# Two more raw buffers for the up weights of the context half of a SwiGLU feed-forward

## The chip, the cores and the metric

The program runs on one core of one Trainium2 chip. The core has a TensorE (PE in the profile, with its weight loads shown as PEld), a VectorE (DVE), a ScalarE (ACT), a GpSimd (POOL) and a SyncE (SP), which work on their own instruction queues and meet at semaphores, and 16 DMA engines that move data between HBM and on-chip SBUF. The metric is the device time of one execution in microseconds (us); lower is better.

## The reference

A backbone trunk of two layers over 1024 latent tokens and a prefix of 256 context tokens, model width 1024. Each layer has a mixing part (grouped attention beside a bidirectional Mamba-2 scan, one shared input and one shared output projection) and a SwiGLU feed-forward of width 2816. In the first layer both streams are updated; in the second only the latent one. The part that matters here is the feed-forward:

```python
D_FF = -(-8 * D_MODEL // (3 * 256)) * 256          # 2816

def swiglu(h, w_gate, w_up, w_down):
    return (jax.nn.silu(h @ w_gate) * (h @ w_up)) @ w_down
...
        if update_ctx:
            x_ctx = x_ctx + g1_c * rmsnorm(m_c, norm_mix_post[l])
            f_c = rmsnorm(x_ctx, norm_ffn_pre[l]) * (1.0 + sc2_c) + sh2_c
            x_ctx = x_ctx + g2_c * rmsnorm(swiglu(f_c, w_gate[l], w_up[l], w_down[l]), norm_ffn_post[l])
```

All inputs are float32.

## The kernel before

**Arithmetic.** Every matrix product in float32 is made of three PE passes over numbers in a shorter float format. An operand is split into hi, the rounded number, and lo, what is left. `split` does this with two instructions: hi is an ACT copy (a CAST, L114), lo is a subtraction (L115) on DVE or POOL. `mm3` then issues hi by hi, hi by lo and lo by hi (L224, L225, L226).

**Weights.** `plan` lists all weight units of the program in the order in which PE wants them, and `pump` emits them. `unit` (from L119) makes one: it takes a raw tile `raw_t` of 128 x 1024 floats (4 KB in each partition) from the pool `raw`, which has **two buffers** used in turn, lets SP load it by DMA (L125), takes a split tile `w_t` from the pool `wr`, which has five buffers, and splits the one into the other. `pump` emits unit i only after PE's use of unit i-5 has been written down (`RING = 5`). Which engine makes lo is chosen in `pump`: DVE for keys that hold "z" or "u", POOL for most of the others, gate units among them.

**The stage.** The context part of the first layer's feed-forward is `ctx_gateup` (L1061 on). For each of 22 column blocks `ff` it multiplies one gate unit and one up unit by the context tile `hc`: 8 x 3 matmuls of 128x256 for each unit, 48 for a block, 1056 in all. The units come in the order g0, u0, g1, u1 and so on, so with two raw buffers used in turn the gate units fall on the one and the up units on the other. Then ACT takes silu of the gate result (L1073), DVE multiplies by the up result (L1074), the product is split into `xt` and stored to `hid` by an ACT-issued DMA (L1077). After each block `next(fill, None)` issues one step of `fill_c`, the preparation of the latent half: it flips two latent token tiles (`flip_steps`, L398 to L408), loads rows of the residual stream (`row_halves`, L376, tile `s2t`), and forms the sums of `quads` (L1005 to L1032), 32 PE transposes (L1012) with ACT, DVE and POOL work and DMAs of its own. When block 21 is done, `ffn` makes the latent half of the same layer; its weights are again raw tiles (`wblock`, L205 loads, L213 to L216 sums on DVE, then splits).

**Memory.** Pools are opened and closed as a stack. `accp` is the pool of this stage and of the latent half that follows; it lies where the pools of the attention lay, which are closed by then. `grp` has one buffer with tag `grow`; in the attention's output projection it holds the gate row (read by L828), later in `ffn` the tile `head_g` of block 3, and after it the gate row of the down projection.

**Order.** The code is written in one sequence. A scheduler with a model of time then moves instructions within each engine's queue, and places the waits for buffers. So a change in buffers can change the order on every engine, also far behind the place of the edit.

Of the kernel before, what the change touches and what calls it, by code (L numbers as in the profile page):

```python
# [9 lines left out]
F32 = mybir.dt.float32  # L10
# [7 lines left out]
P = 128  # L18
# [36 lines left out]
class Trunk:  # L55
    def __init__(self, nc, tc, es, I, out):
# [24 lines left out]
        d = lambda name, shape: self.dr.tile(shape, F32, name=name)  # L81
# [11 lines left out]
        self.hf_d = [d(f"hf{l}", [KT // 2, 2, P, 512]) for l in range(DEPTH)]  # L93
        self.b22_d = d("b22", [KT // 4, 2, P, 512])
        self.hid_d = [d(f"hid{l}", [NFF, P, 2, TOK]) for l in range(DEPTH)]
        self.cols, self.last_x = {}, {}


    def psw(self):
# [16 lines left out]

    RING = 5

    def unit(self, parts, shape, dst=None, eng=None):  # L119
        nc = self.nc  # L120
        n = int(np.prod(shape))
        r = self.raw.tile([P, 1024], F32, tag="raw", name="raw_t")
        rv = r[:, :n].rearrange("p (a b) -> p a b", a=shape[0])
        for sl, ap in parts:
            nc.sync.dma_start(rv[:, :, sl], ap)  # L125
        w = dst if dst is not None else self.wr.tile([P, 2, 1024], F32R, tag="w", name="w_t")
        self.split(w[:, 0, :n], w[:, 1, :n], r[:, :n], eng)
        return w[:, :, :n].rearrange("p s (a b) -> p s a b", a=shape[0])
# [43 lines left out]
    def pump(self):  # L172
        while self.nemit < len(self.seq):
            i = self.nemit
            if i >= self.RING and self.seq[i - self.RING][0] not in self.freed:
                return
            key, parts, shape = self.seq[i]
            if shape is None:
                w = self.wr.tile([P, 2, 1024], F32R, tag="w", name="w_t")
                for j, b in enumerate(parts):  # L180
                    self.wblock(w[:, :, j * 512:(j + 1) * 512], *b)
                self.U[key] = w
                self.nemit += 1
                continue
            self.U[key] = self.unit(parts, shape, None, None if key[1] in "zu" or i < 4 or key[2:] == (0, 0) or len(key) == 4 and key[:3] == (1, "d", 2) and key[3] % 2 else self.nc.gpsimd)
            self.nemit += 1

    def free(self, *key):
# [891 lines left out]
    def ffn(self, l, B, fill, accp=None, xs0=None, xs1=None):  # L1080
        nc = self.nc

        def mul(p, ff, a, b):
            n, j = self.wpos[l, ff, a]
            w = self.U[l, "w", n][:, :, j * 512:(j + 1) * 512]
            for k in range(4):
                s = slice(k * P, (k + 1) * P)
                self.mm3(p, (w[:, 0, s], w[:, 1, s]), (B[b][:, k, 0], B[b][:, k, 1]), k == 0, k == 3)
            if j:
                self.free(l, "w", n)  # L1090
# [11 lines left out]
        def head(ff):  # L1102
            if ff == 3:
                g = self.grp.tile([P, D], F32, tag="grow", name="head_g")
                x1, sa = g[:, 0:512], g[:, 512:1024]
            else:
                x1, sa = [accp.tile([P, 512], F32, name=f"head{i}") if ff == 2 else self.s2() for i in range(2)]
            a = self.psw()
            mul(a, ff, "A11", "B11")
            nc.scalar.copy(x1, a)  # L1110
            a = self.psw()
            mul(a, ff, "A12", "B21")
            fill()
            tt(sa, x1, a, op=ALU.add)
            nc.scalar.activation(sa, sa, AF.Silu)
            st[ff] = x1, sa
# [37 lines left out]
        if heads:  # L1154
            for _ in self.quads(l, xs0, 0, B):
                pass
            head(0)
            self.pre_scale(xs1)
            head(1)
            for _ in self.quads(l, xs1, 1, B):  # L1160
                pass
            head(2)
            head(3)
            third(0)
# [67 lines left out]
def emit(nc, tc, I, out, dump=None):  # L1232
    with ExitStack() as es:
        k = Trunk(nc, tc, es, I, out)
# [18 lines left out]
        for l in range(DEPTH):  # L1253
# [62 lines left out]
            with tc.tile_pool(name=f"acc{l}", bufs=1, reuse_waits="tile") as accp:  # L1316
                if l == 0:
                    B = {}

                    def fill_c():  # L1320
                        fl[2]()
                        yield
                        xs = [k.row_halves(t, 0) for t in (6, 7)]
                        B.update(k.blocks(accp))
                        yield
                        for i in range(2):
                            k.pre_scale(xs)
                            yield
                            for _ in k.quads(0, xs, i, B):
                                yield  # L1330
                            if i == 0:
                                xs = [k.row_halves(t, 0) for t in (8, 9)]
                                yield

                    fc = fill_c()
                    k.ctx_gateup(0, fc)
                    drain(fc)
# [57 lines left out]
```

## Time and profile before

| what | value |
|---|---|
| three runs, us | 3227.97 (median), 3227.72, 3238.06 |
| profiled execution, us | 3234.53, of which its span is 3232.7 |
| granted PE clock, mean over the span | 0.973 |
| `ctx_gateup`, first to last matmul of `hc` by `w_t` | 855.6 to 1030.5 us |

The profiled execution is one run of its own; its span is counted from its first to its last recorded instruction. A row of the windows view gives for one stretch the length, the busy time of each engine with its number of instructions (x), the granted PE clock as a share of full speed, the busy share of the 16 DMA engines and the rate at which they moved data. A row of a timeline gives start, duration, engine, line, operation and out<-in; in square brackets stands the idle time before and what ended it. The chain of waits goes back from the last instruction of a stretch, at each step to what released it. Names are the kernel's own, without buffer numbers; `SPq` and `ACTq` are DMAs being issued.

### The profile page before, as it was taken

How to read it: one execution, taken by the hardware profiler on the slowest of the kernel's cores; microseconds unless marked ns; L12 is line 12 of the kernel's file. 1: busy time of each engine (PE TensorE's matmuls, PEld its weight loads, DVE VectorE, ACT ScalarE, POOL GpSimd, SP SyncE). 2: the span in 40 equal slices, each digit the busy share in tenths (PEclk: the TensorE clock that was granted, in tenths of full speed). 3: DMA queues.
4: the chain of work that ended last, by engine and by line, in shares of the span. 5: the costliest groups of instructions: out<-in, count | busy, mean ns of one | idle time of the engine just before them, and what ended most of it. 6: DMA issues, size and time to landing. Idle time of an engine off the chain costs nothing.

```text
span 3232.7 us, 44982 instructions
## 1 busy us (share of the span) xinstructions
PE 3041.5 (94%) x16147; PEld 2517.7 (78%) x16147; DVE 1665.7 (52%) x3093; ACT 1410.9 (44%) x2595; POOL 1663.6 (51%) x1529
## 2 busy tenths in 40 slices
PE   6899899999888999999998998899999899999997
PEld 4677688888787777778876778788888688888885
DVE  2557556777553655553021156759665766554003
ACT  4433337667653333332143344337666633333232
POOL 4327465555654444444476643755444555554653
PEclk8899899999999999999999999999999899999999
DMA  6267553222565554446566515653222443336766
GB/s 229 71 216 229 188 171 105 84 66 72 170 207 179 169 189 156 171 170 235 181 227 230 169 51 166 216 172 113 66 66 79 137 131 117 111 110 209 237 241 213
DMA packets 372703, 510.66 MB, mean 158 GB/s; under 512 B 25400, under 2 KB 258520, under 8 KB 372224
## 3 DMA queue, kind: packets, MB, share of 16 engines
q1 hardware_dynamic: 292912, 385.09, 37.9%
q10 hardware_dynamic: 79568, 122.69, 10.3%
q8 instruction: 128, 2.10, 0.3%
q14 instruction: 95, 0.78, 0.1%
HBM read 384.71 MB, written 122.99 MB: 157 GB/s over the span
## 4 chain that ended last, share of the span: by engine, by line
PE 73%; DMA 9%; DVE 6%; POOL 5%; ACT 3%; issue 3%; SPq 0%; ACTq 0%; DVEq 0%; POOLq 0%
PE ps_w L224 11%; PE ps_w L225 11%; PE ps_w L226 11%; PE ps_s L224 7%; PE ps_s L225 7%; PE ps_s L226 7%; PE ps_w L912 5%; PE ps_w L905 4%; PE ps_s L883 4%; POOL w_t L115 3%; DMA raw_t<-in_w_down 2%; DMA raw_t<-in_w_up 2%; ACT w_t L114 1%; PE ps_w L275 1%; PE ps_w L755 1%
## 5 line engine op out<-in xcount | busy, mean ns | idle before, releaser
L115 POOL TENSOR_TENSOR w_t<-raw_t,w_t 128x512 fp32r<-128x512 f32 (+2 forms) x430 | 795.7, 1861 | 834.3 <-ACT w_t L114 806.1
L114 ACT CAST w_t<-raw_t 128x512 fp32r<-128x512 f32 (+2 forms) x490 | 389.3, 810 | 774.4 <-PE ps_s L226 240.5
L884 DVE TENSOR_SCALAR_CACHE_REDUCE att_a<-ps_s 128x512 f32<-128x512 f32 (+1 forms) x400 | 227.0, 586 | 138.4 <-PE ps_s L883 128.1
L892 POOL TENSOR_SCALAR att_a<-att_a,att_st 128x1280 f32<-128x1280 f32 (+1 forms) x144 | 181.7, 1264 | 152.3 <-DVE att_st L891 84.2
L225 PE MATMUL ps_w<-w_t,hid_ring 128*128 128x512 f32 x523 | 207.5, 397 | 8.6 <-POOL w_t L115 8.6
L226 PE MATMUL ps_w<-w_t,hid_ring 128*128 128x512 f32 x523 | 206.3, 395 | 0.0
L224 PE MATMUL ps_w<-w_t,hid_ring 128*128 128x512 f32 x523 | 195.9, 395 | 3.7 <-ACT w_t L114 3.1
L905 PE MATMUL ps_w<-cst_all,att_a 128*128 128x128 f32 x1312 | 198.4, 277 | 0.0
L890 ACT ACTIVATE att_a<-att_a,att_st 128x1280 f32<-128x1280 f32 (+1 forms) x144 | 183.2, 1273 | 32.9 <-DVE att_st L889 30.6
L485 DVE SCALAR_TENSOR_TENSOR xt<-row,convw,xt 128x512 f32<-128x512 f32 (+1 forms) x128 | 125.1, 1031 | 84.5 <-ACT xt L483 66.0
L905 PEld LDWEIGHTS ps_w<-cst_all,att_a 128*128 128x128 f32 x1312 | 153.9, 142 | 10.7 <-DVE xt L828 5.4
L828 DVE SCALAR_TENSOR_TENSOR xt<-ps_w,rstd_t,gate_row 128x512 f32<-128x512 f32 x57 | 40.0, 746 | 230.8 <-POOL rstd_t L232 168.8
L115 DVE TENSOR_TENSOR w_t<-raw_t,w_t 128x1024 fp32r<-128x1024 f32 (+1 forms) x60 | 69.9, 1173 | 168.9 <-ACT w_t L114 168.9
L115 DVE TENSOR_TENSOR xt<-s2t,xt 128x512 fp32r<-128x512 f32 (+2 forms) x144 | 121.7, 846 | 48.2 <-ACT xt L114 46.6
L114 ACT CAST xt<-s2t 128x512 fp32r<-128x512 f32 (+2 forms) x144 | 78.0, 542 | 147.3 <-DVE s2t L1141 61.9
L224 PE MATMUL ps_w<-ha,w_t 128*128 128x512 f32 x352 | 138.5, 394 | 2.3 <-ACT xt L1016 2.3
L225 PE MATMUL ps_w<-ha,w_t 128*128 128x512 f32 x352 | 138.8, 394 | 2.0 <-DVE ha L406 2.0
L226 PE MATMUL ps_w<-ha,w_t 128*128 128x512 f32 x352 | 138.2, 393 | 0.0
L225 PEld LDWEIGHTS ps_w<-w_t,hid_ring 128*128 128x128 f32 x523 | 98.9, 189 | 34.0 <-POOL w_t L115 12.0
L224 PE MATMUL ps_w<-hc,w_t 128*128 128x256 f32 x352 | 106.1, 302 | 19.6 <-ACT w_t L114 17.6
L224 PEld LDWEIGHTS ps_w<-w_t,hid_ring 128*128 128x128 f32 x523 | 98.7, 189 | 26.8 <-ACT w_t L114 4.0
L226 PEld LDWEIGHTS ps_w<-w_t,hid_ring 128*128 128x128 f32 x523 | 98.9, 189 | 21.4
(364 smaller groups left out, 8771.3 us busy)
## 6 DMA issues: line engine op xcount, KB each, us to landing
raw_t<-in_w_down SPq DMA_DIRECT2D x132, 512.0 KB
hid<-xt ACTq DMA_DIRECT2D x88, 512.0 KB
raw_t<-in_w_gate SPq DMA_DIRECT2D x70, 512.0 KB
raw_t<-in_w_up SPq DMA_DIRECT2D x66, 512.0 KB
hid_ring<-hid SPq DMA_DIRECT2D x85, 384.0 KB
xt<-in_w_mod SPq DMA_DIRECT2D x56, 512.0 KB
xt<-xs SPq DMA_DIRECT2D x36, 512.0 KB
raw_t<-in_w_in SPq DMA_DIRECT2D x32, 512.0 KB
```

Source lines behind the costliest of these rows:

```text
L114: self.nc.scalar.copy(hi, src)
L115: (eng or self.nc.vector).tensor_tensor(lo, src, hi.bitcast(F32), op=ALU.subtract)
L224: mm(out, st[0], mv[0], start=first, stop=False)
L225: mm(out, st[0], mv[1], start=False, stop=False)
L226: mm(out, st[1], mv[0], start=False, stop=last)
L485: nc.vector.scalar_tensor_tensor(acc, row[:, o0 + k:o0 + k + n], cw[:, ct, k:k + 1], acc, op0=ALU.mult, op1=ALU.add)
L883: nc.tensor.matmul(s[:, :m], qs[t][c][:, hd], kst[:, g, j:j + m], start=c == 0, stop=c == 1)
L884: nc.vector.tensor_scalar(pb[:, j:j + m], s[:, :m], -0.125, None, op0=ALU.mult, op1=ALU.min, accum_out=st[:, n:n + 1])
L890: nc.scalar.activation(pb, pb, AF.Exp, bias=nmx, scale=-1.0, accum_out=st[:, 4:5])
L892: nc.gpsimd.tensor_scalar(pb, pb, st[:, 5:6], 1.0, op0=ALU.mult, op1=ALU.mult)
L905: nc.tensor.transpose(tp[:, (2 * k + h) * P:(2 * k + h + 1) * P], pr[h][:, (k2 + k) * P:(k2 + k + 1) * P], self.ident)
L912: nc.tensor.matmul(av, vst[:, kt, g], pt[:, c, k * 256:(k + 1) * 256], start=kt == 0 and c == 0, stop=kt == nk - 1 and c == 1)
```

## The change

Units may now be given their raw tile by the caller. From the opening of the stage `ctx_gateup` on, the up units take turns between two tiles of their own, both called `raw_u`: even blocks one in `accp` (a new tag of that pool), odd blocks one in `grp` under the tag `grow`. The pool `raw` with its two buffers is then left to the gate units of this stage. The first five units of the stage (g0, u0, g1, u1, g2) are emitted before `spare` is set and use the pool `raw` as before. The room in `accp` is that of two tiles `head0` and `head1`, which block 2 of the latent half took from `accp` in both layers; in the first layer block 2 now takes two tiles `s2t` of the common pool, as its neighbours do. The number of units, DMAs, splits and matmuls stays.

```diff
-        self.cols, self.last_x = {}, {}
+        self.cols, self.last_x, self.spare = {}, {}, ()
...
-    def unit(self, parts, shape, dst=None, eng=None):
+    def unit(self, parts, shape, dst=None, eng=None, r=None):
         nc = self.nc
         n = int(np.prod(shape))
-        r = self.raw.tile([P, 1024], F32, tag="raw", name="raw_t")
+        if r is None:
+            r = self.raw.tile([P, 1024], F32, tag="raw", name="raw_t")
...
+            r = None
+            if key[1] == "u" and self.spare:
+                r = self.spare[key[3] % 2]()
...
-                x1, sa = [accp.tile([P, 512], F32, name=f"head{i}") if ff == 2 else self.s2() for i in range(2)]
+                x1, sa = [accp.tile([P, 512], F32, name=f"head{i}") if l and ff == 2 else self.s2() for i in range(2)]
...
+                    k.spare = (lambda: accp.tile([P, 1024], F32, tag="raw", name="raw_u"),
+                               lambda: k.grp.tile([P, 1024], F32, tag="grow", name="raw_u"))
                     fc = fill_c()
                     k.ctx_gateup(0, fc)
```

The edit adds lines, so L125 of the kernel before is L126 after it, L376 is L380, L988 is L992, L213 is L217, L1074 is L1078.

On SP, at the start of the stage, the loads stood in this order before (the pair of `xt` loads is two latent token tiles for the flips, `s2t` are residual rows for the quads, `hf` are kept flips):

```order
L125 DMA raw_t<-in_w_gate 128x8x128
L125 DMA raw_t<-in_w_up 128x8x128
L988 DMA xt<-xs_95 128x1024 x2
L125 DMA raw_t<-in_w_gate 128x8x128
L125 DMA raw_t<-in_w_up 128x8x128
L376 DMA s2t<-xs_95 128x512
L125 DMA raw_t<-in_w_gate 128x8x128
L376 DMA s2t<-xs_95 128x512 x2
L125 DMA raw_t<-in_w_up 128x8x128
L376 DMA s2t<-xs_95 128x512
```

Now they stand so. Both lists begin with the loads of block 2:

```order
L126 DMA raw_u<-in_w_up 128x8x128
L126 DMA raw_t<-in_w_gate 128x8x128 x2
L992 DMA xt<-xs_95 128x1024 x2
L126 DMA raw_u<-in_w_up 128x8x128
L126 DMA raw_t<-in_w_gate 128x8x128
L126 DMA raw_u<-in_w_up 128x8x128
L126 DMA raw_t<-in_w_gate 128x8x128
L380 DMA s2t<-xs_95 128x512 x3
L126 DMA raw_u<-in_w_up 128x8x128
L380 DMA s2t<-xs_95 128x512
```

The up load of block 2 stands before both gate loads, two gate loads instead of a gate and an up load stand before the pair of `xt` loads, and two more weight loads stand before the first rows `s2t`; the last row stands behind one up load in both.

On DVE, at the end of the stage and the start of the latent half, the rows before were these (L115 with `w_t` is the lo of an up unit, L1074 the product of a block, L213 to L216 the sums of the latent half's first block):

```order
L115 TENSOR_TENSOR w_t<-raw_t,w_t 128x1024
L115 TENSOR_TENSOR xt<-s2t,xt 128x256
L115 TENSOR_TENSOR w_t<-raw_t,w_t 128x1024
L213 TENSOR_TENSOR s2t<-raw_t 128x512
L1074 TENSOR_TENSOR s2t<-s2t,ps_w 128x256
L214 TENSOR_TENSOR raw_t<-raw_t 128x512
L215 TENSOR_TENSOR raw_t<-raw_t 128x512
L115 TENSOR_TENSOR xt<-s2t,xt 128x256
L216 TENSOR_TENSOR raw_t<-raw_t 128x512
```

And now:

```order
L115 TENSOR_TENSOR w_t<-raw_u,w_t 128x1024
L1078 TENSOR_TENSOR s2t<-s2t,ps_w 128x256
L217 TENSOR_TENSOR s2t<-raw_t 128x512
L115 TENSOR_TENSOR xt<-s2t,xt 128x256
L218 TENSOR_TENSOR raw_t<-raw_t 128x512
L219 TENSOR_TENSOR raw_t<-raw_t 128x512
L220 TENSOR_TENSOR raw_t<-raw_t 128x512
L1078 TENSOR_TENSOR s2t<-s2t,ps_w 128x256
```

The last lo of an up unit has moved ahead of the product before it, and all four sums of the latent half's first block now stand before the next product.

Behind the latent half of the first layer the order is the same on all engines up to the query projection of the second layer, where pieces of the Mamba-2 part (`ssd_x`, L699 after the change) fill in. There SP had, before:

```order
L854 DMA att_c<-k_106 128x2560
L670 DMA xt<-ea_110 20x1024
L695 DMA ssd_x<-xtok_100 128x768
L737 DMA ssd_S<-bt_112 8x2x128 x6
```

and now:

```order
L858 DMA att_c<-k_106 128x2560
L699 DMA ssd_x<-xtok_100 128x768
L674 DMA xt<-ea_110 20x1024
L741 DMA ssd_S<-bt_112 8x2x128 x6
```

One load of `ssd_x` has passed the load of `ea`; on PE, DVE, ACT and POOL some dozens of rows in the same stretch are interleaved otherwise.

More of the change, by code (lines that the diff above doesn't have):

```diff
@@ L184, in pump @@
                 continue
-            self.U[key] = self.unit(parts, shape, None, None if key[1] in "zu" or i < 4 or key[2:] == (0, 0) or len(key) == 4 and key[:3] == (1, "d", 2) and key[3] % 2 else self.nc.gpsimd)
+            r = None
+            if key[1] == "u" and self.spare:
+                r = self.spare[key[3] % 2]()
+            self.U[key] = self.unit(parts, shape, None, None if key[1] in "zu" or i < 4 or key[2:] == (0, 0) or len(key) == 4 and key[:3] == (1, "d", 2) and key[3] % 2 else self.nc.gpsimd, r)
             self.nemit += 1
```

## The prediction

> **What bounds the kernel now.** The page comes first: which engine is full, and how long the profiled execution is.
>
> ```profile
> span 3232.7 us, 44982 instructions
> PE 3041.5 (94%) x16147; PEld 2517.7 (78%) x16147; DVE 1665.7 (52%) x3093; ACT 1410.9 (44%) x2595; POOL 1663.6 (51%) x1529
> ```
>
> PE is the bound overall, so a change of buffers can only win where PE stands still or runs at a low clock. The stage that is edited is the next thing to look at. I cut it in the windows view where its character changes: the start (855.55), the first matmul of unit 3 (876.9), the last transposes of the quads (929.05), the end of the quads' tail (961.4), the end of the stage (1030.7). The latent half follows.
>
> ```profile
> core 0: us, PE busy (x) PEld busy (x) DVE busy (x) ACT busy (x) POOL busy (x), PEclk, DMA share, GB/s
> 855.55:876.90 21.35, 15.00 (x90) 14.52 (x88) 10.76 (x11) 11.55 (x22) 11.66 (x14) 0.73 0.79 260
> 876.90:929.05 52.15, 49.28 (x392) 48.39 (x392) 34.66 (x40) 34.36 (x69) 35.43 (x34) 0.97 0.77 244
> 929.05:961.40 32.35, 24.18 (x170) 22.67 (x169) 19.45 (x25) 16.13 (x28) 15.13 (x8) 0.91 0.62 189
> 961.40:1030.70 69.30, 58.69 (x459) 57.28 (x459) 16.96 (x26) 24.23 (x36) 22.04 (x11) 0.97 0.58 171
> 1030.70:1060.00 29.30, 26.98 (x119) 19.58 (x118) 18.73 (x23) 10.83 (x21) 16.90 (x13) 0.94 0.58 195
> 1060.00:1200.00 140.00, 139.94 (x699) 103.92 (x698) 80.14 (x104) 47.04 (x83) 66.69 (x50) 1.00 0.52 176
> ```
>
> The counts are the point. Busy time flatters PE here, because matmuls overlap; what a full PE needs is read from the distance of their starts.
>
> ```profile
> 870.62 0.42 PE L226 MATMUL ps_w<-hc,w_t 128*128 128x256 f32 x1
> 870.84 0.42 PE L224 MATMUL ps_w<-hc,w_t 128*128 128x256 f32 x1
> ...
> 1030.35 0.28 PE L225 MATMUL ps_w<-hc,w_t 128*128 128x256 f32 x1
> 1030.47 0.28 PE L226 MATMUL ps_w<-hc,w_t 128*128 128x256 f32 x1
> ```
>
> At full clock one starts every 0.12 us; right after a pause it is 0.21 to 0.22. So each pause costs itself and some slow matmuls behind it. With 0.12 us for every instruction counted, the second window needs 392 x 0.12 = 47.0 of its 52.15, the third 20.4 of 32.35, the fourth 55.1 of 69.30. What a never waiting PE would save is **5.1, 11.9 and 14.2 us, 31.2 together**. In the window behind the stage PE stands 2.3 us and the clock is 0.94, at most 4.1 us; from 1060 on it is full.
>
> What ends the waits in the fourth window, the chain shows:
>
> ```profile
> by line: DMA raw_t<-in_w_up 56.1%; DVE w_t L115 12.2%; ACT w_t L114 10.5%; PE ps_w L224 6.4%; PE ps_w L226 6.0%; PE ps_w L225 5.7%; issue 2.0%; DVE s2t L213 1.6%; DVE xt L115 0.2%; DVE s2t L1074 0.2%; ACTq L114 0.2%; DVEq L1074 0.1%; DVEq L
> ...
> 965.50 1.22 DVE w_t L115
> 966.75 4.17 DMA raw_t<-in_w_up
> 970.99 1.05 ACT w_t L114
> 972.07 1.22 DVE w_t L115
> 973.32 4.91 DMA raw_t<-in_w_up
> ...
> 1011.28 5.96 DMA raw_t<-in_w_up
> ...
> 1024.96 1.24 DVE w_t L115
> ```
>
> This is a loop through **one buffer**: load an up unit, hi, lo, and only then the next load into the same place. From the lo at 965.50 to that at 1024.96 it goes round 8 times, 7.4 us for a block; PE needs 48 x 0.12 = 5.8 us for a block. The up buffer, not PE, sets the pace.
>
> **The change part by part.** The sum is made against the profiled execution, 3234.53 us (span 3232.7 and 1.8 around it). That is 6.6 above the median of the runs, 3227.97; the same saving is taken off the median at the end. No instruction is added or removed; two tiles of one pool become two of another. So everything comes from waits.
>
> *Last window, 961.4 to 1030.7.* The costs of a block by engine:
>
> ```profile
> L115 POOL TENSOR_TENSOR w_t<-raw_t,w_t 128x1024 fp32r<-128x1024 f32 x9 | 21.5, 2388 | 47.7 <-ACT w_t L114 47.7
> L114 ACT CAST w_t<-raw_t 128x1024 fp32r<-128x1024 f32 x17 | 17.8, 1047 | 35.9 <-DMA raw_t<-in_w_up 16.5 <-DMA raw_t<-in_w_gate 15.9 <-DVE xt L115 3.5
> L115 DVE TENSOR_TENSOR w_t<-raw_t,w_t 128x1024 fp32r<-128x1024 f32 x9 | 11.0, 1223 | 13.2 <-ACT w_t L114 13.2
> L1073 ACT ACTIVATE s2t<-ps_w 128x256 f32<-128x256 f32 x9 | 3.4, 377 | 3.0 <-PE ps_w L226 3.0
> L1074 DVE TENSOR_TENSOR s2t<-s2t,ps_w 128x256 f32<-128x256 f32 x8 | 3.4, 421 | 37.9 <-PE ps_w L226 33.6 <-issue 4.3
> L115 DVE TENSOR_TENSOR xt<-s2t,xt 128x256 fp32r<-128x256 f32 x8 | 3.3, 418 | 0.0
> L114 ACT CAST xt<-s2t 128x256 fp32r<-128x256 f32 x8 | 3.2, 403 | 3.4 <-DVE s2t L1074 3.4
> ```
>
> ACT 2 x 1.05 + 0.38 + 0.40 = 2.9 us, POOL 2.4, DVE 1.22 + 0.42 + 0.42 = 2.1, all under 5.8. With two buffers each, the up loop is 7.4 / 2 = 3.7 us for a block; the gate loop, with POOL's 2.4 in place of DVE's 1.2, about (2.4 + 1.05 + 5) / 2 = 4.2. What is late next is PE itself. The load of an up unit may now start when the unit two blocks back has its lo. The five `w_t` buffers let the splits run five units (5 x 2.9 = 14 us) ahead of PE, so the load has four units, 11.5 us, less the splits' 3.4, that is 8 us, against the 4.2 to 6.0 in the chain. I take **13 of the 14.2**. Lower end 8: if each load were stretched to 9 us by the others in flight, the loops would come to 5.7 and 6.2, and the gate loop would just bind.
>
> *Third window, 929.05 to 961.4.* The same loop, but the quads' DVE, ACT and POOL work and loads lie between. If second and third window shrank to PE's need, 84.5 us would become 67.4. DVE's 54.1 us in them would then fill 80%, ACT's 50.5 and POOL's 50.6 some 75%, and the data (52.15 x 244 + 32.35 x 189, 18.8 MB) would have to move at 280 GB/s. That the DMA engines do more with these loads, the start of the stage shows:
>
> ```profile
> 860.00:865.00 5.00, 3.66 (x30) 3.45 (x28) 4.62 (x4) 2.51 (x3) 1.11 (x1) 0.97 0.92 342
> ```
>
> So nothing is full, but queues served in order at 80% do cause waits. I take **8 of the 11.9**, between 3 and 11.9.
>
> *Second window.* PE loses little here, since it lives on five split units that lay ready at 876.9; with the new buffers up to four more raw units are loaded by then. I take **2.5 of 5.1**, between -1 and 5.1.
>
> *Start, 855.55 to 876.9.* PE waits there for the pair of `xt` loads.
>
> ```profile
> 853.53 0.37 SPq L125 DMA_DIRECT2D raw_t<-in_w_gate  x1
> 854.61 0.37 SPq L125 DMA_DIRECT2D raw_t<-in_w_up  x1
> 855.41 1.24 SPq L988 DMA_DIRECT2D xt<-xs  x2
> ...
> 862.45 0.38 SPq L125 DMA_DIRECT2D raw_t<-in_w_gate  x1
> ...
> 864.80 0.38 SPq L125 DMA_DIRECT2D raw_t<-in_w_up  x1
> ```
>
> In SP's new order the load at 854.61 becomes that of g3, which needs the same buffer (freed by u1), so the pair stays at 855.4. Block 2's up load moves ahead of 853.53, into a stretch where little is moved. Behind the pair, block 3's up load need not wait for 864.80 any more; it and g4 then compete with the pair, which cannot gain and may lose a transfer's time. I take **0**, between -3 and +1. The wait of block 3's load is new: the `grow` tile's last reader before it is L828, whose last pair ends at 857.0.
>
> ```profile
> 855.58 1.41 DVE L828 SCALAR_TENSOR_TENSOR xt<-ps_w,rstd_t,gate_row 128x512 f32<-128x512 f32 x2 [0.99 <-POOL rstd_t L232]
> ```
>
> SP is done with the pair at 856.7, so this holds it for some 0.3 us, and behind it stand only loads that came later than 857 before.
>
> *Behind the stage.* The raw pool now holds g20 and g21 only, so the latent half's first gate and up loads start after the lo of those, some 14 us ahead of PE, and DVE's four sums stand ahead of the last product. Of the 4.1 us there I take **1.5**, between -3 and 4.1. Block 2's `head` tiles cost nothing: PE is full from 1060 on (139.94 of 140.00) and covers them; without that cover, by estimate, two waits of the length of a DVE sum (0.42 us in L1074's row).
>
> *Second layer.* The reordered stretch is one where PE already waits:
>
> ```profile
> 2000.00:2050.00 50.00, 45.58 (x212) 37.07 (x213) 41.20 (x80) 19.62 (x33) 33.00 (x32) 0.93 0.52 168
> 2050.00:2100.00 50.00, 41.30 (x199) 33.17 (x198) 37.09 (x44) 16.35 (x28) 36.55 (x31) 0.97 0.73 254
> ...
> PEld ps_w L592 <- issue: 8.1, 3, 4.8
> PE ps_w L592 <- DVE xt L115: 6.9, 3, 4.4
> ```
>
> 13.1 us of idle PE in 100. The same pieces interleaved otherwise may move that by a wait of this size in either direction: **0**, between -5 and +5.
>
> Sum: 13 + 8 + 2.5 + 0 + 1.5 + 0 = **25 us**: 3234.5 becomes 3209.5, and the median 3228 becomes **3203**. All low ends together give -1, all high ends 41; since they are separate matters, I hold 18 to 33 for this case, 3195 to 3210.
>
> **The rivals.** *The quads set the pace (gain 9 to 17, time about 3214).* Then the second and third windows stay as they are, and only the last gives its 13, with 1 behind it. For it: DVE, ACT and POOL are each at 65 to 68% of the second window already, and their work hangs together. Against it: the waits in the third window end in the same up loads and splits. The Trainium skill has a rule that would bring this about: by "SBUF — State Buffer", section "Who interferes with whom", a DVE instruction with two SBUF inputs and a GpSimd instruction that reads SBUF shut each other out for their whole length. The lo subtractions are of that kind on both engines; taken in full, the rule would leave DVE and POOL no room to run closer together in the quads, and the time would be this rival's. The trace bears it out only in part: in the second window DVE's and POOL's busy times add up to 70.1 us in 52.15, so they do overlap for 18.
>
> *The loads do not start earlier (gain under 9, about 3224).* SP works in order; if each up load stands behind a gate load that waits for POOL's lo, the new buffers lie empty. Against it: the gate loop also has two buffers, 4.2 us a block.
>
> *Slower: the second layer's new order.* Place: the query projection with the Mamba-2 pieces, 2000 to 2100. Eight latent tiles pass there; if each paid one wait like the longest there, 4.8 us, that would be 38 us, 25 come back, and the time is 3228 + 13 = 3241. It decides from 25 + 9.7 = 35 us on, 4.3 us for each tile. Against it: only three such waits stand there now, and the rows moved by a place or two.
>
> **How the numbers follow.** A measurement of this kernel can tell about 0.3%, 9.7 us, from no change. Forecast 0.72, quads 0.16, no earlier loads 0.08, slower 0.04. Faster by over 0.3%: the forecast and most of the quads' case, 0.86; within: 0.10; slower: 0.04. The range takes the forecast's 3195 to 3210 and reaches over most of the quads' case, down by one for its own low side: **3194 to 3217**.
>
> **What would show it.** Right: the stage, from its first to its last `hc` matmul, takes about 151 us in place of 175; from its unit 25 on the starts keep 0.12 us; the chain there is PE's, with no `in_w_up` load; the wait of ACT's CAST for raw loads (16.5 and 15.9 us in the last window) is near nothing; up loads are issued over 10 us ahead of their hi. Quads' case: PE pauses stay between units 15 and 25. Wrong: the stage is short but the latent half starts with a pause of over 5 us, or 2000 to 2100 grows by over 5 us.

## The result, and the profile after

| | before | after |
|---|---|---|
| median, us (8 runs each, taken together) | 3232.26 (3227.72 to 3244.53) | 3215.07 (3203.62 to 3221.36) |
| ratio of the times | | 0.9937, 95% interval 0.9921 to 0.9953 |
| profiled execution, us | 3234.53 | 3221.04 |
| first to last matmul of `hc` by `w_t`, us | 174.9 | 156.8 |

The change makes the kernel faster by 0.6%, some 17 to 21 us. The predicted 3203 is 12 us too low: 4 of them because the kernel before ran at 3232.3 in these runs and not at 3228, 8 because 17 us came back and not 25. The time lies inside the predicted range.

The page of after. Of the 13.4 us by which the spans differ, PE's busy time gives 6.7, and the other half was idle time.

```profile
span 3219.3 us, 45016 instructions
PE 3034.8 (94%) x16147; PEld 2511.3 (78%) x16147; DVE 1679.0 (52%) x3093; ACT 1410.2 (44%) x2595; POOL 1668.3 (52%) x1529
```

The windows of after begin at the same places of the program as those of before: start of the stage, unit 3, unit 18, unit 25, end of the stage. The last is 29.30 us long, as there.

```profile
core 0: us, PE busy (x) PEld busy (x) DVE busy (x) ACT busy (x) POOL busy (x), PEclk, DMA share, GB/s
861.55:883.60 22.05, 15.20 (x90) 14.68 (x88) 12.58 (x11) 11.45 (x23) 11.46 (x14) 0.72 0.90 295
883.60:942.30 58.70, 49.47 (x393) 48.24 (x393) 40.24 (x41) 37.48 (x71) 41.38 (x36) 0.97 0.78 242
942.30:963.90 21.60, 21.60 (x169) 21.60 (x170) 20.34 (x24) 14.16 (x25) 11.79 (x7) 0.93 0.57 176
963.90:1018.70 54.80, 54.80 (x459) 54.80 (x458) 34.74 (x32) 25.35 (x42) 26.64 (x13) 1.00 0.68 201
1018.70:1048.00 29.30, 29.30 (x144) 22.39 (x143) 15.42 (x22) 9.81 (x19) 16.28 (x12) 1.00 0.69 235
```

Read the lengths against those of before. The last window holds the same 459 matmuls in 54.80 us in place of 69.30, with PE busy throughout at full clock. The third fell from 32.35 to 21.60. **The second grew from 52.15 to 58.70**, with the same 392 or 393 PE instructions. Behind the stage, 29.30 us now hold 144 PE instructions where they held 119.

What PE waits for from 861.5 to 1020, summed by the wait (us in total, times, the longest), the three longest:

```profile
PE ps_w L402 <- POOL xt L375: 6.1, 1, 6.1
PE ps_w L1016 <- POOL s2t L375: 4.7, 3, 4.1
PE ps_w L1016 <- ACT xt L1020: 4.3, 1, 4.3
```

The first is the pair at the stage's start, which stood there before as well (5.6 us). Waits for weights (`w_t`) are gone. New are two waits of the transposes in the quads (L1016), both in the second window.

The groups of the last window:

```profile
L115 POOL TENSOR_TENSOR w_t<-raw_t,w_t 128x1024 fp32r<-128x1024 f32 x8 | 19.2, 2401 | 25.2 <-DVE w_t L115 19.8 <-ACT w_t L114 5.4
L115 DVE TENSOR_TENSOR xt<-s2t,xt 128x256 fp32r<-128x256 f32 x10 | 18.1, 1806 | 4.3 <-ACT xt L114 4.3
L115 DVE TENSOR_TENSOR w_t<-raw_u,w_t 128x1024 fp32r<-128x1024 f32 x8 | 9.8, 1226 | 14.0 <-ACT w_t L114 14.0
L114 ACT CAST w_t<-raw_u 128x1024 fp32r<-128x1024 f32 x8 | 8.4, 1047 | 21.5 <-DVE xt L115 13.7 <-PE ps_w L230 7.9
L114 ACT CAST w_t<-raw_t 128x1024 fp32r<-128x1024 f32 x8 | 8.3, 1041 | 1.2 <-DVE xt L115 1.2
```

ACT's CASTs wait for no load any more (16.5 and 15.9 us before). Most of the up CAST's wait now ends with DVE's lo of `xt` (the 7.9 us put down to PE are three waits of the same 2.6 us in the last blocks), and that lo takes 1.81 us on average where it took 0.42 before. This row looks harmless, since PE is full; behind the stage it turned out to matter.

The second window's two pauses in the timeline, PE, ACT, POOL, DVE and SP:

```profile
927.29 0.33 PE L1016 MATMUL ps_w<-cst_all,s2t 128*128 128x128 f32 x1 [4.10 <-POOL s2t L375]
941.34 0.66 PE L1016 MATMUL ps_w<-cst_all,s2t 128*128 128x128 f32 x4 [4.26 <-ACT xt L1020]
...
939.32 1.04 ACT L114 CAST w_t<-raw_t 128x1024 fp32r<-128x1024 f32 x1 [2.70 <-DMA raw_t<-in_w_gate]
940.27 1.93 ACT L1020 ACTIVATE xt<-ps_w,cols 128x256 f32<-128x256 f32 x4
...
925.57 2.33 POOL L375 TENSOR_SCALAR s2t<-s2t,rstd_t 128x512 f32<-128x512 f32 x2
927.87 2.55 POOL L115 TENSOR_TENSOR w_t<-raw_t,w_t 128x1024 fp32r<-128x1024 f32 x1
...
929.03 2.47 DVE L115 TENSOR_TENSOR w_t<-raw_u,w_t 128x1024 fp32r<-128x1024 f32 x1 [0.86 <-ACT w_t L114]
...
913.54 1.97 SPq L380 DMA_DIRECT2D s2t<-xs  x4
...
926.70 5.20 SPq L126 DMA_DIRECT2D raw_u<-in_w_up  x2
931.99 1.01 SPq L1009 DMA_DIRECT2D xt<-hf  x2
933.05 1.69 SPq L126 DMA_DIRECT2D raw_t<-in_w_gate  x2
```

The first pause waits for the rescaled rows of the second pair of tiles (L375). Their loads (L380) were issued at 913.54, 51.9 us behind the stage's start; before, it was 48.5 us behind it (904.07). On SP they now stand behind the gate load of block 9, which waits for its buffer until 913.07; before, they stood behind the loads of block 7. The second pause waits for PSUM that ACT empties (L1020). L1020 stands on ACT behind a gate CAST, the gate CAST waits for its load, and the load was issued at 933.05, although POOL's lo had freed its buffer at 930.42 (927.87 + 2.55): on SP two up loads stand ahead (926.70 and 931.53), and the second of them had to wait for its own buffer, that is for DVE's lo that ends at 931.50 and took 2.47 us, beside POOL's of 927.87, where this lo takes 1.22 alone. So the quads' work came later: their second pair's first transpose 65.6 us behind the stage's start in place of 61.5. PE came to it no earlier than before, 61.4 us behind the start.

The second layer's stretch, 2000 to 2100 in before, in after:

```profile
1988.61:2039.31 50.70, 47.38 (x213) 38.49 (x213) 39.50 (x79) 19.76 (x33) 32.48 (x32) 0.90 0.51 164
2039.31:2085.98 46.67, 40.15 (x198) 31.98 (x197) 35.56 (x43) 15.71 (x26) 34.73 (x29) 1.00 0.78 264
```

97.4 us. In before, from the same first to the same last PE instruction, it is 99.3 (2000.9 to 2100.2). So the new order costs nothing here. At most half of the 2.0 us lasts: at the instruction that stands at 2150 in before, the three profiles of after have gained -0.2 to 1.0 us since 2000.

### The profile page after: what moved, and what is told of

It reads as the page before. It is cut to its first block, busy times and chain, and to the rows that moved or that the text cites. A ratio compares the mean times of both kernels' runs of the same rounds, so it can differ in the third digit from the quotient of the medians.

```text
span 3219.3 us, 45016 instructions
## 1 busy us (share of the span) xinstructions
PE 3034.8 (94%) x16147; PEld 2511.3 (78%) x16147; DVE 1679.0 (52%) x3093; ACT 1410.2 (44%) x2595; POOL 1668.3 (52%) x1529
## 4 chain that ended last, share of the span: by engine, by line
PE 51%; DMA 6%; POOL 4%; DVE 4%; ACT 2%; issue 2%; ACTq 0%; SPq 0%; DVEq 0%; POOLq 0%
PE ps_w L228 9%; PE ps_w L229 9%; PE ps_w L230 9%; PE ps_s L228 5%; PE ps_s L229 5%; PE ps_s L230 5%; DMA raw_t<-in_w_down 3%; POOL w_t L115 2%; PE ps_w L916 2%; PE ps_w L909 2%; PE ps_s L887 2%; ACT w_t L114 1%; PE ps_w L279 1%; DMA raw_t<-in_w_up 0%; PE ps_w L759 0%
## 5 line engine op out<-in xcount | busy, mean ns | idle before, releaser
L115 POOL TENSOR_TENSOR w_t<-raw_t,w_t 128x512 fp32r<-128x512 f32 (+2 forms) x430 | 797.4, 1865 | 812.2 <-ACT w_t L114 766.1
L114 ACT CAST w_t<-raw_t 128x512 fp32r<-128x512 f32 (+2 forms) x470 | 368.2, 799 | 715.2 <-PE ps_s L230 249.0
L115 DVE TENSOR_TENSOR xt<-s2t,xt 128x512 fp32r<-128x512 f32 (+2 forms) x145 | 141.2, 975 | 57.7 <-ACT xt L114 55.5
L909 PEld LDWEIGHTS ps_w<-cst_all,att_a 128*128 128x128 f32 x1312 | 153.2, 141 | 11.3 <-DVE xt L832 5.5
L115 DVE TENSOR_TENSOR w_t<-raw_t,w_t 128x1024 fp32r<-128x1024 f32 (+1 forms) x40 | 44.2, 1116 | 141.2 <-ACT w_t L114 141.2
L887 PE MATMUL ps_s<-att_c,raw_q 128*128 128x512 f32 (+1 forms) x400 | 109.3, 372 | 7.2 <-DMA raw_q<-q 6.8
L230 PEld LDWEIGHTS ps_w<-w_t,hid_ring 128*128 128x128 f32 x523 | 98.7, 189 | 21.5
```

Of the source, the lines that this page charges most:

```text
L114: self.nc.scalar.copy(hi, src)
L115: (eng or self.nc.vector).tensor_tensor(lo, src, hi.bitcast(F32), op=ALU.subtract)
L230: mm(out, st[1], mv[0], start=False, stop=last)
L887: nc.tensor.matmul(s[:, :m], qs[t][c][:, hd], kst[:, g, j:j + m], start=c == 0, stop=c == 1)
L909: nc.tensor.transpose(tp[:, (2 * k + h) * P:(2 * k + h + 1) * P], pr[h][:, (k2 + k) * P:(k2 + k + 1) * P], self.ident)
```

## The experiments

For every profiled run the same lengths are taken from the starts of PE's matmuls: the stage's four windows, the next 119 PE instructions (the start of the latent half), and the sum. Where the quads come later, 16 of their transposes lie in the third window and no longer in the second, so there these two are compared by their sum. "Load" is the time from the stage's end to the issue of the latent half's fourth weight load (the up weights of its block 1). The last columns are the difference of the medians to the kernel before on the same chip, and the ratio with its 95% interval.

| kernel | start | second | third | last | 119 | sum | load | us | ratio |
|---|---|---|---|---|---|---|---|---|---|
| before | 21.4 | 52.3 | 32.2 | 69.0 | 29.7 | 204.6 | +9.8 | | |
| after | 22.0 | 58.6 | 21.6 | 54.6 | 25.0 | 181.8 | +3.0 | -17.2 | 0.9937 (0.9921 to 0.9953) |
| after, again | 22.7 | 58.4 | 22.0 | 54.6 | 25.2 | 182.9 | +3.2 | -19.4 | 0.9949 (0.9931 to 0.9966) |
| after, third | 21.9 | 58.7 | 21.8 | 54.6 | 25.0 | 182.0 | +3.0 | -20.8 | 0.9931 (0.9919 to 0.9943) |
| 1 head tiles only | 20.7 | 52.8 | 28.4 | 72.2 | 28.2 | 202.3 | +8.1 | +4.0 | 1.0013 (0.9995 to 1.0032) |
| 2 one buffer | 20.4 | 56.3 | 20.3 | 62.7 | 31.3 | 191.0 | +8.9 | -10.1 | 0.9968 (0.9948 to 0.9988) |
| 3 quads later | 20.6 | 45.1 | 30.4 | 54.6 | 30.7 | 181.4 | +8.3 | -19.0 | 0.9945 (0.9926 to 0.9964) |
| 4 before, quads later | 19.9 | 49.4 | 30.2 | 70.8 | 30.6 | 200.9 | +10.6 | +1.3 | 1.0004 (0.9994 to 1.0014) |
| 5 quads later, one load moved | 20.5 | 45.8 | 32.9 | 56.3 | 28.9 | 184.4 | +6.4 | -18.9 | 0.9939 (0.9927 to 0.9951) |
| 6 one load moved | 20.6 | 58.1 | 21.5 | 54.6 | 25.8 | 180.6 | +4.7 | -21.9 | 0.9921 (0.9900 to 0.9942) |
| 7 quads later, stores on SP | 21.7 | 45.6 | 32.4 | 54.9 | 25.0 | 179.6 | +1.4 | -21.7 | 0.9937 (0.9923 to 0.9950) |
| 8 quads later, gate lo on DVE | 21.7 | 45.4 | 30.0 | 54.6 | 25.0 | 176.7 | +1.2 | -24.6 | 0.9921 (0.9908 to 0.9935) |
| 8 again | 22.3 | 45.7 | 28.8 | 54.6 | 25.0 | 176.4 | +1.2 | -22.4 | 0.9933 (0.9909 to 0.9958) |
| 9 stores on SP, from block 10 | 21.5 | 59.0 | 21.4 | 54.6 | 25.0 | 181.5 | +1.3 | -15.9 | 0.9954 (0.9941 to 0.9967) |

The windows repeat to within 1.2 us from profile to profile of one kernel, the medians only to some 4 us. So what a few us did is read from the windows, and the times say whether it arrives.

### After, again

> The changed kernel once more, beside the others on one chip. Theory (the one up buffer set the pace; with two, PE keeps 0.12 us a matmul from unit 18 on, and what is left of the waits is PE standing at the transposes of the second pair of the quads): stage, first to last hc matmul, 155 to 159 us in place of 175; time 18 to 23 us under the kernel before. Rival (the quads' pauses were chance of one profiled execution): stage below 150 us.

> The changed kernel once more, as the measure for the others of this call. Both theories: 10 to 23 us under the kernel before, ratio 0.993 to 0.997, stage 156 to 158 us, the pauses of 4 to 5 us at its units 16 and 18 again.

Stage 157.7 and 157.0 us, with pauses of 3.66 and 4.28, 3.27 and 4.80 us at units 16 and 18. They belong to the order of this kernel, not to one execution.

### 1 and 2: what of the change does it

One takes the two buffers away and leaves the moved head tiles; two gives only the even up units a tile of their own.

```diff
-                    k.spare = (lambda: accp.tile([P, 1024], F32, tag="raw", name="raw_u"),
-                               lambda: k.grp.tile([P, 1024], F32, tag="grow", name="raw_u"))
```
```diff
-                               lambda: k.grp.tile([P, 1024], F32, tag="grow", name="raw_u"))
+                               lambda: None)
```

> Only the two head tiles of block 2 taken from the common pool; the up units keep the raw pool's one buffer. Theory (all gain is from the buffers): stage 174 to 176 us, time within 5 us of the kernel before. Rival (part of the gain is from the head tiles or from another order behind the stage): time more than 8 us lower with the stage at 175.

> One more buffer in place of two: even up units in the stage's region, odd ones in the raw pool, which then sees three units in two blocks for its two buffers. Theory (a loop of about 7.7 us for each unit through each buffer): 3 x 7.7 / 2 = 11.6 us for two blocks, 5.8 for one, which is just PE's pace; the tail behind unit 25 takes 55 to 59 us (69 before, 54.6 after), stage 156 to 162, time 14 to 22 us under the kernel before. Rival (a load's latency grows with every one more in flight, or both buffers are needed): tail 61 us or more, gain under 12 us.

Without the buffers the stage is back at 174.3 us and the time at that of before: all of the gain is the buffers'. One of them brings 10.1 us. Its last window, 62.7, is about midway between 69.0 and 54.6, and behind the stage it pays 31.3 in place of 25.0. The window and the 10.1 us are those that its rival named, not its theory. Which of the rival's two reasons holds, loads that take longer the more are in flight or a need for both buffers, was not separated; in this window ACT's CASTs still wait 8.1 us for up loads and 7.9 for gate loads. So the second buffer, in the gate row's place, is worth the other half, and much of that comes at the start of the latent half.

### 3 and 4: the quads' place

Two empty steps after the loads of the second pair of rows, in the kernel after (3) and in the kernel before (4).

```diff
                                 xs = [k.row_halves(t, 0) for t in (8, 9)]
                                 yield
+                                yield
+                                yield
```

> The changed kernel, with two empty steps between the loads of the second pair of rows and the rest of their quads, so that PE meets their transposes at units 20 and 22 in place of 16 to 18. Theory (PE stood 4.4 and 4.5 us there because rows and ACT's evacuation came late in their queues, not because an engine was full): the two pauses go or shrink below 1 us each, stage 146 to 151 us, time 6 to 10 us under the changed kernel. Rival (DVE and POOL cannot run closer together in the quads, so the work takes its time wherever it stands): pauses of the same length at the new place, stage 155 to 159, time as the changed kernel's.

> The kernel before, with only the quads' second pair two steps later (transposes at units 20 and 22), and no new buffers. Theory (the one up buffer sets the pace of the stage's second half; the quads' order matters only once it is gone): the stage stays within 3 us of 175, its last 60 to 70 us as before, and the time within 5 us of the kernel before. Rival (the quads' place alone would have brought much of the gain): the stage falls to 168 us or less, and the time by 6 us or more.

In the kernel before it changes the time by nothing (ratio 1.0004), though its profile shows a stage 4.6 us shorter, a little more than the 3 that were expected: while one buffer sets the pace, the quads' place decides little. In the kernel after, the two pauses of the second window go: second and third window take 75.5 us together in place of 80.2, the stage 150.7 in place of 157, within what was expected. So PE's new pauses came of the quads' lateness; what it still waits for in the third window are 2.84 and 1.61 us, for PSUM that silu and product empty. But the time, expected 6 to 10 us lower, stays that of after: **the next 119 PE instructions take 30.7 us in place of 25.0**. In the timeline behind the stage of this run (it ends at 994.4):

```profile
1006.83 0.50 PE L228 MATMUL ps_w<-h_t,w_t 128*128 128x512 f32 x1 [3.93 <-ACT s2t L1077]
...
1005.36 1.14 ACT L114 CAST w_t<-raw_t 128x512 fp32r<-128x512 f32 x2 [5.04 <-DMA raw_t<-in_w_gate]
1006.40 0.38 ACT L1077 ACTIVATE s2t<-ps_w 128x256 f32<-128x256 f32 x1
...
997.02 5.67 POOL L115 TENSOR_TENSOR w_t<-raw_t,w_t 128x512 fp32r<-128x512 f32 x4
...
987.91 0.37 SPq L209 DMA_DIRECT2D raw_t<-in_w_up  x1
1001.48 0.37 SPq L209 DMA_DIRECT2D raw_t<-in_w_gate  x1
```

PE waits for ACT's silu of the last context block, the silu stands behind a CAST, the CAST waits for block 1's gate load, and that was issued at 1001.48, when POOL was through with the weights in its buffer.

### 5 and 6: is it that one buffer?

The latent half's first up weights go into the up units' tile in `accp`, so that the gate load of block 1 need not wait for POOL.

```diff
-                st[kind] = self.raw.tile([P, 1024], F32, tag="raw", name="raw_t")
+                st[kind] = self.spare[0]() if self.spare and kind == "u" and (l, ff) == (0, 0) else self.raw.tile([P, 1024], F32, tag="raw", name="raw_t")
```

> The changed kernel, with the quads' second pair two steps later, and with one more load given its own place: the first up weights of the latent half (its block 0) are loaded into the up units' tile in accp instead of the raw pool, so that block 1's gate weights need no longer wait until POOL has made four lo from block 0's up weights. Theory (the 6 to 7 us that the shorter stage won were given back at the latent half's start through this one buffer: load at 1001.48, ACT's CAST waits for it 5.04 us, ACT's silu of the last context block behind the CAST, PE 3.93 us): the stage stays at 150 to 152 us, the first 119 PE instructions behind it take 25 to 27 us in place of 30.7, the first 600 122 to 124 in place of 127.4, and the time is 4 to 7 us under that of the changed kernel in this call. Rival (the latent half's start is bound by the data that must come in before it, whatever the place): the 119 stay at 29 to 31 us, and the time within 2 us of the changed kernel's.

> The changed kernel with only the place of that one load changed (block 0's up weights of the latent half into the up units' tile in accp), the quads as in the change. In the changed kernel's own trace the same wait just fits (PE comes to its need 0.7 us after ACT's silu). Theory: nothing to win here, the 119 PE instructions behind the stage keep 24 to 26 us, the stage 156 to 159, the time within 2 us of the changed kernel's. Rival (the load's place counts by itself): the 119 fall by over 2 us, and the time by as much.

**This theory fell.** The load came early, but the 119 still take 28.9 us, the time does not move, and the stage, 155.5 us, missed the 150 to 152 as well. What PE waits for in 5 from 1000 to 1034 (the second wait lies before the stage's end at 1015.6), and SP's loads there:

```profile
PE ps_w L279 <- DMA xt<-in_w_mod: 2.5, 1, 2.5
PE ps_w L230 <- DVE w_t L115: 1.5, 1, 1.5
```
```profile
1003.43 0.37 SPq L209 DMA_DIRECT2D raw_u<-in_w_up  x1
1005.86 0.37 SPq L209 DMA_DIRECT2D raw_t<-in_w_gate  x1
1022.00 0.37 SPq L209 DMA_DIRECT2D raw_t<-in_w_up  x1
...
1024.51 1.73 SPq L302 DMA_DIRECT2D xt<-in_w_mod  x3
```

The wait only moved on: now block 1's up load (1022.00) comes 6.4 us behind the end, and the loads of `in_w_mod` stand behind it on SP. In the table the 119 go by this load's place: up to 3.2 us behind the end they take 25.0 to 25.2, at 4.7 us 25.8, and from 6.4 us on 28 to 31. So the question was not which buffer, but why the whole queue of splits and loads is 5 us nearer to PE in 3 than in after. Six brought what was expected of it, 25.8 us for the 119 and a time 1 us under that of after beside it; its stage, 154.9, is 1 us shorter than expected.

### 7, 8 and 9: the loop that PE hides

The answer stands in after's own timeline, in a block of the last window: ACT, DVE, POOL and SP.

```profile
984.91 1.05 ACT L114 CAST w_t<-raw_u 128x1024 fp32r<-128x1024 f32 x1 [2.62 <-DVE xt L115]
...
987.58 0.41 ACT L114 CAST xt<-s2t 128x256 fp32r<-128x256 f32 x1 [0.40 <-DVE s2t L1078]
989.99 0.52 ACTq L1081 DMA_DIRECT2D hid<-xt  x1
990.63 1.05 ACT L114 CAST w_t<-raw_u 128x1024 fp32r<-128x1024 f32 x1 [2.64 <-DVE xt L115]
...
985.99 1.22 DVE L115 TENSOR_TENSOR w_t<-raw_u,w_t 128x1024 fp32r<-128x1024 f32 x1 [1.75 <-ACT w_t L114]
987.14 0.41 DVE L1078 TENSOR_TENSOR s2t<-s2t,ps_w 128x256 f32<-128x256 f32 x1
988.02 1.94 DVE L115 TENSOR_TENSOR xt<-s2t,xt 128x256 fp32r<-128x256 f32 x1 [0.47 <-ACT xt L114]
...
987.26 2.42 POOL L115 TENSOR_TENSOR w_t<-raw_t,w_t 128x1024 fp32r<-128x1024 f32 x1 [3.31 <-DVE w_t L115]
...
975.80 0.37 SPq L126 DMA_DIRECT2D raw_u<-in_w_up  x1
```

Follow it by the times: up CAST 984.91, up lo 985.99, product 987.14, CAST of `xt` 987.58, lo of `xt` 988.02 to 989.96, ACT's store that waits for this lo 989.99, next up CAST 990.63. None of these steps waits for PE. The loop takes **5.72 us, PE's block 5.77**. So behind the quads the splits cannot gain on PE, and what lead they have at the end is what they had at the quads. In after the splits went on while PE stood in its two pauses: the last up CAST comes 8.0 us ahead of its unit (1007.7 and 1015.7); in 3, without the pauses, 2.8 us. Of the loop, 1.5 us are what the lo of `xt` takes beyond its 0.42: it ends 0.28 us after POOL's lo of the gate unit (989.68), as in every block there.

Seven issues the stores from SP from block 12 on; eight lets DVE make the gate lo from block 13 on; both with the quads later. Nine issues the stores from SP from block 10 on (`ff > 9` in place of `ff > 11`), with the quads where the change has them.

```diff
-            nc.scalar.dma_start(self.hid_d[l][ff, :, :, 0:CTX], hd.bitcast(F32))
+            (nc.sync if ff > 11 else nc.scalar).dma_start(self.hid_d[l][ff, :, :, 0:CTX], hd.bitcast(F32))
```
```diff
-... key[2:] == (0, 0) or ...
+... key[2:] == (0, 0) or key[1] == "g" and key[3] >= 13 or ...
```

> The changed kernel, the quads' second pair two steps later, and the stores of the product to hid issued by SP instead of ACT from block 12 on. Theory (behind the quads, ACT and DVE go round one loop of 5.70 us for a block: up CAST, up lo, product, CAST of xt, lo of xt that DVE ends only when POOL's lo is done (1.92 us in place of 0.42), ACT's store that waits for it, next up CAST; PE's 5.77 us just hide it, so the splits never get further ahead of PE, and what lead they lack at the end is paid at the latent half's start): without the store on ACT the loop is about 3.5 us, the last up CAST comes 6 to 11 us ahead of its unit in place of 2.9, the stage stays at 149 to 152 us, the first 119 PE instructions behind it fall from 30.7 to 24 to 27 us, and the time is 4 to 8 us under the changed kernel's, 23 to 29 under the kernel before. Rival (the latent half's start is bound by its own loads and POOL's lo's): the 119 stay at 29 to 31, the time within 2 us of the changed kernel's, 18 to 22 under the kernel before.

> The changed kernel, the quads' second pair two steps later, and the gate units' lo of blocks 13 and later made by DVE in place of POOL. Theory of the 5.70 us loop: with POOL quiet, DVE's lo of xt is back at 0.41 to 0.45 us, the loop is about 4.2 us, though DVE now makes two lo in a block (1.22 each); the last up CAST comes 6 to 11 us ahead, the 119 fall to 24 to 27, and the time is 4 to 8 us under the changed kernel's. If DVE and POOL do not hold each other up, the lo of xt stays at 1.9 us. Rival (its own loads bind the latent half's start): the 119 stay at 29 to 31, the time within 2 us of the changed kernel's.

> The changed kernel with the quads where the change has them, and the stores of the product to hid issued by SP instead of ACT from block 10 on. Theory of the 5.70 us loop: the splits get further ahead than 8.1 us here too, but the pauses of 4 to 5 us at units 16 and 18 came before and stay, and PE ran without a pause behind them already: stage 155 to 158, the 119 at 23 to 25.5, the time 0 to 3 us under the changed kernel's. Rival (the store on SP holds the loads back in SP's order): the stage's end or the 119 grow by over 2 us, the time is over that of the changed kernel.

> The changed kernel with the quads' second pair two steps later and the gate units' lo of blocks 13 and later on DVE, once more. Theory (its stage and the first 119 PE instructions behind it take 176 to 178 us together, the changed kernel's 182 to 183): 22 to 28 us under the kernel before, ratio 0.9915 to 0.993. Rival (the 24.6 us of the first comparison were a good draw): a ratio of 0.994 or more, as the changed kernel's own.

In both 7 and 8 the last up CAST comes 11 us ahead and the 119 fall from 30.7 to 25.0: breaking the loop at either of two quite different points gives the lead back. The rival falls. The chain of waits through the last window shows the same. In the second profile of after (948.7 to 1003.3) its largest part is the lo of `xt`; in the other two it enters the window only 5 us before the end. In 7 and 8 it is PE's alone, here 8 from 950.4 to 1005:

```profile
by line: DVE xt L115 28.3%; issue 18.3%; ACT w_t L114 16.8%; POOL w_t L115 8.3%; ACTq L1081 7.7%; DMA raw_t<-in_w_up 7.6%; ACT xt L114 5.3%; DVE s2t L1078 4.7%; DVE w_t L115 2.6%; DVE s2t L217 1.3%; ACTq L114 0.5%; ACT s2t L1077 0.3%; DVEq 
```
```profile
by line: PE ps_w L229 33.4%; PE ps_w L230 33.4%; PE ps_w L228 33.4%
```

Eight in the timeline:

```profile
970.00 1.05 ACT L114 CAST w_t<-raw_u 128x1024 fp32r<-128x1024 f32 x1 [0.42 <-DMA raw_u<-in_w_up]
973.95 1.05 ACT L114 CAST w_t<-raw_u 128x1024 fp32r<-128x1024 f32 x1 [0.31 <-DMA raw_u<-in_w_up]
...
971.08 1.23 DVE L115 TENSOR_TENSOR w_t<-raw_u,w_t 128x1024 fp32r<-128x1024 f32 x1 [0.22 <-ACT w_t L114]
973.37 1.23 DVE L115 TENSOR_TENSOR w_t<-raw_t,w_t 128x1024 fp32r<-128x1024 f32 x1 [0.73 <-ACT w_t L114]
974.51 0.42 DVE L115 TENSOR_TENSOR xt<-s2t,xt 128x256 fp32r<-128x256 f32 x1
```

With POOL quiet, the lo of `xt` is back at 0.42 us, a block takes 3.95 here, and the CASTs wait for loads again, with room to spare; in the last blocks they wait for PE to give back a `w_t` buffer, at a lead of 11.3 us. The sum is 176.4 and 176.7, 5 to 6 us under that of after. In the times 8 is 24.6 and 22.4 us under the kernel before, after 17.2, 19.4 and 20.8: in the expected direction and at the low end of what was expected, in the repeat a little beyond it (0.9933 where 0.993 was the end). The intervals overlap, so the times alone do not show that 8 beats after; the windows do, for this part of the program. Seven missed in two points: its stage is 4 us longer than that of 3 (start 1 us, third window 2), and its time no better than after's. Nine gains nothing in the windows, as expected; its time is at after's or above it, as its rival had it, but not for the rival's reason, since neither the stage's end nor the 119 grew. It loses 5.6 us in the second layer: at PE's instruction that stands at 2100 in before it is 22.7 us ahead of before, at that of 2150 it is 17.1. Why was not followed up.

## Why the prediction was right, and where not

| step | predicted gain, us | measured in the windows |
|---|---|---|
| last window | 13 (8 to 14.2) | 14.5 (69.30 to 54.80) |
| third window | 8 (3 to 11.9) | 10.8 (32.35 to 21.60) |
| second window | 2.5 (-1 to 5.1) | **-6.6 (52.15 to 58.70)** |
| start | 0 (-3 to 1) | -0.7 |
| behind the stage | 1.5 (-3 to 4.1) | 4.7 (29.7 to 25.0 for 119) |
| second layer | 0 (-5 to 5) | 2.0 (99.3 to 97.4) |

**The main step was right.** One up buffer set the pace, two remove it: from unit 25 on 459 matmuls take 54.80 us, PE waits for no weights there, and experiment 1 shows that nothing else in the change moves the time. The up loads are issued 9.1 us ahead of their CAST (975.80 to 984.91), not quite the 10 that were named, and the lead of the CASTs over PE is 7.6 to 9.6 us there, not the five units, 14 us, that were reckoned with. One sign did not come: the chain of waits through this window, in the second profile, is not PE's but the loop of ACT and DVE. The prediction added up a block's work engine by engine, 2.9, 2.4 and 2.1 us, all well under PE's 5.8, and left out that these steps wait for each other: the chain through them takes 5.72.

**The step that failed is the second window**, "I take 2.5 of 5.1, between -1 and 5.1". It was bounded by what PE lost there, as if the work beside it would keep its times. The quads' row loads were issued 3.4 us later in SP's new order, their last evacuations stood on ACT behind a CAST whose load came late, and PE lost 4.1 and 4.3 us in two new waits, though it came to the first of them no earlier than before. The sign that was named for the rival "quads set the pace", PE pauses between units 15 and 25, appeared; but the third window, which that rival would have left as it was, gained 10.8. The quads moved the loss into the second window and kept 4.7 us of the two windows together (experiment 3), not the 10.5 that the rival gave them. The stage came to 157 and not 151 for this reason; the third and the last window, 2.8 and 1.5 us better than forecast, made up for a part. That the windows still add up to the 25 of the forecast is luck: the 9.1 us missed in the second window and 0.7 at the start are about what these two, the latent half's start and the second layer brought beyond theirs.

**The rule on SBUF was set aside on a wrong reading.** The prediction held against it that DVE's and POOL's busy times overlap for 18 us. After shows that a busy row contains the time in which the instruction is held: the lo of `xt` has 1.94 us beside POOL's lo and 0.42 without it (experiment 8). The window that the prediction summed had such rows itself. This one stands beside POOL's lo from 881.55 to 884.27 and ends 0.28 us after it:

```profile
881.93 2.62 DVE L115 TENSOR_TENSOR xt<-s2t,xt 128x256 fp32r<-128x256 f32 x1
```

In the second window of after DVE's busy time is 5.6 us longer than before, of which one more lo of an up unit makes 1.2; of POOL's 6.0, two more subtractions of 2.4 us make 4.8. So in these rows POOL's subtraction holds up DVE's. The Trainium skill states in "SBUF — State Buffer", section "Who interferes with whom", that a DVE instruction with two SBUF inputs contends with a GpSimd instruction that reads SBUF. The trace agrees, 1.94 us against 0.42, and the overlap of busy times said nothing against it. What the rule costs in the second window was not measured by itself; experiment 3 shows that it did not bind there as the rival had it, since the two pauses went when the quads came later.

**Behind the stage** the gain was 4.7 and not 1.5, and over the bound of 4.1. The raw pool without up units, the reason that was given, is not enough: experiment 3 has it too, and its 119 take 30.7. The size depends on the lead that ACT has over PE at the end of the stage. In experiment 2, with one buffer less, this gain is absent.

**The sum.** The table's measured terms add up to 25, as predicted; the profiled pair differs by 13.5. Of the rest, 6.0 us are lost before the stage begins (861.6 against 855.6), where PE has the same instructions in the same order, 3.6 us between 1700 and 1800, which the other two profiles of after do not lose, and at most half of the second layer's 2 us lasts. The medians, 17 to 21 us lower, lie between. Why they stay 4 to 8 us under the windows' 25 is not settled. One reason may be that the kernel before was profiled once: experiments 1 and 4, whose times are those of before, have sums of 202.3 and 200.9 in place of 204.6, and against these after's 181.8 to 182.9 are 18 to 21 us. Executions of one kernel spread by up to 25 us (3203.6 to 3221.4 in after's first comparison, 3221.6 to 3246.6 for the kernel before in another), and a median of 4 to 12 runs keeps some of that.

## What to carry to other kernels

When one wait is removed, don't bound the neighbours by what PE loses there now: ask in the new order of every queue when each piece of side work becomes ready. Here a load that waits for its buffer held all loads behind it on SP, and the quads' rows came 3.4 us later. A loop between two other engines that is only just shorter than PE's block cost nothing here while PE was full, but it froze their lead, and the next stage paid for a lead that was too short; read such loops by following one block from CAST to CAST. A busy row may contain time in which another engine held the instruction: compare the duration of the same shape elsewhere before concluding that two engines overlap.

## What was not expected of the hardware

The time to a place in the program has two values, before anything that was edited. At PE's matmul number 750 four of fourteen profiles, of four different kernels, stand at 161 to 162 us, the other ten, before and after among them, at 172 to 175. What PE waits for from 117 to 175 us shows the difference. The third profile of after has this wait, the second has only a wait that both have:

```profile
PE ps_w L279 <- DMA raw_m<-in_w_mod: 8.9, 1, 8.9
```
```profile
PE ps_w L498 <- ACT xt L490: 2.4, 1, 2.4
```

One load of the modulation weights is in time in the four profiles, and PE waits 8.7 to 10.3 us for it in the ten, in executions of the same program. At this place two executions of one kernel so differ by 11 to 14 us, more than half of what the change brings; a single pair of profiles must be compared stretch by stretch.

DVE's lo of 128x256 took 0.42 us alone. Beside a 2.4 us subtraction on POOL it took 1.91 to 1.97 in seven of eight blocks of after's last window and 2.42 in the first, and it ended 0.28 us after POOL's in each.
